# Output projection of a hybrid decoder layer: its buffers, the place of the second norm's weights, and three operands instead of four made beside it

## The chip, the cores and the metric

The kernel runs on one core of a Trainium2 chip. The metric is the device time of one execution in microseconds (us); several runs are shown by their median. One further execution was recorded by the hardware profiler, and all rows below are from that one.

## What is computed

One layer on 2048 tokens of width 1024, in float32: a norm, a projection to four mixers (a gated unit, causal pooling, sliding-window attention, stick-breaking attention), a norm of each mixer's output, the output projection with a residual, a second norm, a SwiGLU feed-forward with a residual, and a last norm.

```python
ycat = jnp.stack([y_a, y_b, y_c, y_d], axis=2)
ycat = _rmsnorm(ycat, mix_out_gain[l].reshape(N_MIXERS, GROUP_WIDTH))
x = x + ycat.reshape(B, S, D_MODEL) @ w_out[l]
h = _rmsnorm(x, norm_ffn[l])
gate, up = jnp.split(h @ w_gate_up[l], 2, axis=-1)
x = x + (jax.nn.silu(gate) * up) @ w_down[l]
return _rmsnorm(x, norm_final)
```

## The kernel before

Float32 products are made of three reduced-precision ones: each operand is split into a high part (a cast on ACT) and the rest (a subtraction on DVE), and TensorE multiplies high by high, high by rest and rest by high. The program is traced by a framework whose scheduler sets the order on each engine from its own timing model, and waits on tiles come from buffer pools: a tile of a tag that has n buffers waits until the one whose place it takes is done with.

Three parts concern us. The **output projection** (`out_proj`) goes over 16 blocks of 128 tokens. `prepare(b)` loads the mixers' rows y (L638) and the residual x (L640), squares y in four groups on ACT (L644), gets the factors from GpSimd (L145), scales y on DVE (L648), turns it by eight TensorE transposes (L630) and splits it into yT (L632 on ACT, L633 on DVE). Then 48 matmuls (L694 to L696) run in two halves, each added to the residual (L697). `finish(b)` stores the new residual, norms it (`normed`: squares L150, factor, scaling L153, written into y's buffer), turns it (L663), copies it to hs (L664) and stores that to DRAM (hTd). The program prepares block b+1 ahead of the matmuls of block b. Sliding-window attention, whose rows y the projection needs, is woven into the first half of these blocks.

The **operands of the gate product**: the feed-forward uses a Strassen-like scheme with seven operands (T2, B11, T3, T1, B21, T4, B22), sums and differences of quarters of the normed, turned rows. In `finish` of four late blocks, b1 and b2 are loaded from hTd, and `put_h` casts (L908) and splits (L909) four of the operands; B21, T4 and B22 are made by `operands` (L960 to L967) when the projection ends. All loads and stores go through one queue, that of SyncE, in order.

The **gate passes** (`gate_up`, 44 of them, 84 matmuls each, L992) and **down passes** (`down`, 88) then take their tiles from one ring, tag k4, of 18 buffers of 4 KB per partition. The projection's weights wo stand in 16 of these, and their raw rows oraw in what is left; fraw is a loaded gate weight, fsum a sum of two, fw a split one, hb and ht the rows and differences for `operands`, ar a loaded activation.

Of the kernel before, what the change touches and what calls it, by code (L numbers as in the profile page):

```python
# [68 lines left out]
def _layout(inputs):  # L69

    f = {k: np.asarray(v, dtype=np.asarray(v).dtype) for k, v in inputs.items()}
    a = {}
    x = f["x"][0]
    a["x"] = x
    a["xT"] = x.T
    w = f["w_in"][0].reshape(KT, P, 2048).transpose(1, 0, 2)

    def cols(*ranges):
        return np.concatenate([w[:, :, lo:lo + n] for lo, n in ranges], 2)

    cm = [cols((o, P)) for o in (D_K, D_Q, B_IN, B_IN + P, D_K + P, D_Q + P, C_K, C_Q, C_Q + P)]
    a["w_cm"] = np.stack(cm, 0)
    a["w_v"] = cols((D_V, 256), (C_V, P))
    a["w_a"] = cols((A_U, 512))
    a["w_out"] = f["w_out"][0]
    gu = f["w_gate_up"][0].reshape(KT, P, 2, NF, P)
    a["w_gu"] = gu.transpose(3, 1, 2, 0, 4)
    a["w_down"] = f["w_down"][0]
    for n in ("norm_mix", "mix_out_gain"):
        a[n] = f[n][0].reshape(KT, P).T  # L90
    a["norm_ffn"] = f["norm_ffn"]
    a["norm_final"] = f["norm_final"][None, :]
    a["sgu_wT"] = f["sgu_w"][0].transpose(2, 0, 1)
    a["sgu_bT"] = f["sgu_b"][0].T
    a["pool_w"] = f["pool_w"][0]
    a["pool_scale"] = f["pool_scale"]
    a["swa_sinks"] = f["swa_sinks"]
    a["rel_bias"] = f["rel_bias"]
    for n, v in _constants().items():
        a["c_" + n] = v  # L100
    return {n: np.ascontiguousarray(v) for n, v in a.items()}
# [13 lines left out]
def _build(nc, tc, A, top):  # L115
    V, S, G = nc.vector, nc.scalar, nc.gpsimd

    def load(out, in_):
        nc.sync.dma_start(out, in_)
# [26 lines left out]

    def normed(pool, x, g, out):

# [3 lines left out]
        rstd(r, ss, D, pool)  # L152
        V.scalar_tensor_tensor(out, x, r, g, op0=ALU.mult, op1=ALU.mult)  # L153

# [3 lines left out]
    with ExitStack() as ph1:  # L158
# [450 lines left out]
        def load_wo():  # L609
# [3 lines left out]
            for k in range(KT):  # L613
                raw = ring.tile([P, 2, CH], F32, name="oraw", tag="k4")
                load(raw, A["w_out"][k * P:(k + 1) * P, :].rearrange("p (n c) -> p n c", n=2))
# [19 lines left out]
        def out_proj(op, wo, put_h):  # L635
            def prepare(b):
                y = op.tile([P, D], F32, name="y", tag="y")
                load(y, yd[b // 2][(b % 2) * P:(b % 2 + 1) * P, :])  # L638
# [8 lines left out]
                for m in range(4):  # L647
                    V.tensor_scalar(y[:, m * 256:(m + 1) * 256], y[:, m * 256:(m + 1) * 256], r[:, m:m + 1], None,  # L648
                                    op0=ALU.mult)
                yT = [op.tile([P, 4, 2, P], F32R, name="yT", tag="yT", bufs=3) for _ in range(2)]  # L650
                split_T(y, yT)
                return y, xr, yT

            def finish(b, y, xr):

                load(x2d[b // 4][(b % 4) * P:(b % 4 + 1) * P, :], xr)
                normed(op, xr, gffn, y)
                hs = op.tile([P, KT, P], F32, name="hs", tag="yT", bufs=3)
                for half in range(2):
                    tr = psum.tile([P, CH], F32, name="ytr", tag="tr")  # L660
                    for k in range(4):
                        kk = half * 4 + k
                        nc.tensor.transpose(tr[:, k * P:(k + 1) * P], y[:, kk * P:(kk + 1) * P], ident)  # L663
                    S.copy(hs[:, half * 4:half * 4 + 4], tr.rearrange("p (k t) -> p k t", k=4))  # L664
                load(hTd[b // NT][:, :, b // 4 % 2, (b % 4) * P:(b % 4 + 1) * P], hs)
                k = b - NT - 1
                if 0 <= k < 4:
                    b1 = op.tile([P, 2, CH], F32, name="b1", tag="y")
                    load(b1, hTd[0][:, k])
                    b2 = op.tile([P, 2, CH], F32, name="b2", tag="xres")  # L670
                    load(b2[:, 0], hTd[0][:, 4 + k, 1])
                    put_h("B11", k, b1[:, 0])
                    V.tensor_tensor(b1[:, 0], b1[:, 1], b1[:, 0], op=ALU.subtract)
                    put_h("T1", k, b1[:, 0])
                    V.tensor_tensor(b1[:, 1], b2[:, 0], b1[:, 1], op=ALU.subtract)
# [215 lines left out]
        alone[0] = 1  # L891
        ring = top.enter_context(tc.tile_pool(name="ring", bufs=18, side="left", reuse_waits="tile"))
        wo = []
# [8 lines left out]
        with tc.tile_pool(name="ph3", bufs=2, side="right", reuse_waits="tile") as p3:  # L902
            fh = top.enter_context(tc.tile_pool(name="fh", bufs=1, side="left", reuse_waits="tile"))
            hc = {n: fh.tile([P, 4, 2, CH], F32R, name=n) for n in ("T2", "B11", "T3", "T1")}

# [4 lines left out]

            gffn = fh.tile([P, D], F32, name="gffn", tag="g")
            load(gffn, A["norm_ffn"].broadcast_to([P, D]))
            need = 0
# [13 lines left out]
    with ExitStack() as ph4:  # L927
        fp = ph4.enter_context(tc.tile_pool(name="fp", bufs=2, side="right", reuse_waits="tile"))
        for n in ("B21", "T4", "B22"):
            hc[n] = fp.tile([P, 4, 2, CH], F32R, name=n, bufs=1)  # L930
        gfin = fh.tile([P, D], F32, name="gfin", tag="g")
        load(gfin, A["norm_final"].broadcast_to([P, D]))
# [94 lines left out]
        def down(c, beside):  # L1027
            tags = (("ms", 1), ("acc", 1), ("mm", 2), ("mm", 2), ("z", 2), ("z", 2), ("tr", 2), ("tr", 2))
            pss = [psum.tile([P, CH], F32, name="dn", tag=t, bufs=n) for t, n in tags]
            for f in range(NF):  # L1030
                if f % 2 == 0:
                    ar = pair("ar")
                    for u in range(2):
                        load(ar[:, u], actd[c][f + u])
# [32 lines left out]

        for k in range(4):
            operands(0, k, ("B21", "T4", "B22"))
        for blk in range(T // TB):  # L1070
# [19 lines left out]
```

## Time and profile before

| | us |
|---|---|
| median of 3 runs | 2517.16 (2516.94 to 2519.28) |
| the profiled execution | 2518.81 |
| its span | 2517.1 |
| mean granted TensorE clock, share of full | 0.951 |
| TensorE busy | 2286.6 (91%) |
| DVE busy | 1623.0 (64%) |
| ACT busy | 1048.7 (42%) |

A busy share is a mean over stages with different limits, so the rows are by stage: where TensorE is full only fewer or faster matmuls help, and where it is not, the row to look for is the wait that ends last. [...] The turning of block 8 begins at 987.15 us, that of block 15 at 1141.06, and the first gate matmul at 1172.49.

### The profile page before, as it was taken

What the parts mean: (1) busy time and instruction counts of PE and PEld (TensorE: products, weight loads), DVE (VectorE), ACT (ScalarE), POOL (GpSimd) and SP (SyncE); (2) the same over time, 40 slices, a digit from 0 to 9 for tenths busy, and PEclk for the clock granted to TensorE, in tenths of its full rate; (3) what the DMA queues carried; (4) which work ended last, traced back from release to release, by engine and by line L of the source; (5) the groups of instructions that cost most, each with busy time, mean ns of one, the idle gap of its engine ahead of it and who ended that gap; (6) DMA issues with size and microseconds to landing.
All of it is one profiled execution on the core that took longest, in us unless ns stands there. A gap on an engine that the chain in (4) does not pass through costs nothing.

```text
span 2517.1 us, 30904 instructions
## 1 busy us (share of the span) xinstructions
PE 2286.6 (91%) x11308; PEld 1926.4 (77%) x11308; DVE 1623.0 (64%) x2634; ACT 1048.7 (42%) x2196; POOL 357.4 (14%) x372
## 2 busy tenths in 40 slices
PE   6989898897886888657999999999999999999998
PEld 6978776776875777545888888888888888888886
DVE  6688999898884543337666666655377666653443
ACT  5455566665654434234333333444233323332332
POOL 4232443454431210000000000000000000000000
PEclk9999999998996999878999999999999999999999
DMA  6232311222314333334222222556432222234553
GB/s 209 68 122 74 100 42 32 63 63 88 107 42 136 110 126 128 120 118 159 96 76 80 85 87 88 156 187 203 156 140 80 76 96 76 80 109 134 168 192 134
DMA packets 148808, 277.32 MB, mean 110 GB/s; under 512 B 12432, under 2 KB 84528, under 8 KB 148656
## 3 DMA queue, kind: packets, MB, share of 16 engines
q1 hardware_dynamic: 148656, 275.34, 32.9%
q8 instruction: 89, 1.46, 0.2%
q14 instruction: 63, 0.52, 0.1%
HBM read 211.60 MB, written 63.70 MB: 109 GB/s over the span
## 4 chain that ended last, share of the span: by engine, by line
PE 66%; DVE 15%; DMA 8%; issue 5%; ACT 3%; POOL 2%; SPq 0%; DVEq 0%; POOLq 0%; ACTq 0%
PE dn L1048 19%; PE gb L992 15%; PE gc L992 10%; PE ga L992 10%; DVE pr L315 4%; DVE s L320 3%; DMA qr<-cd 2%; DMA y<-yd 2%; DVE wt L333 1%; PE ops L694 1%; PE ops L695 1%; PE ps L242 1%; PE ps L243 1%; PE ops L696 1%; PE ps L244 1%
## 5 line engine op out<-in xcount | busy, mean ns | idle before, releaser
L1048 PE MATMUL dn<-wd,act 128*128 128x512 f32 x2112 | 479.5, 389 | 0.0
L1048 PEld LDWEIGHTS dn<-wd,act 128*128 128x128 f32 x2112 | 396.4, 188 | 82.5
L992 PE MATMUL gb<-T,fw 128*128 128x512 f32 x1584 | 387.9, 394 | 11.8 <-ACT fw L980 11.8
L992 PEld LDWEIGHTS gb<-T,fw 128*128 128x128 f32 x1584 | 298.8, 189 | 79.6 <-ACT fw L980 12.2
L992 PE MATMUL ga<-B,fw 128*128 128x512 f32 x1056 | 258.8, 393 | 0.0
L941 DVE TENSOR_TENSOR wd<-wr,wd 128x512 fp32r<-128x512 f32 x176 | 114.7, 689 | 215.4 <-ACT wd L1042 215.3
L992 PEld LDWEIGHTS ga<-B,fw 128*128 128x128 f32 x1056 | 198.6, 188 | 45.2
L145 POOL TENSOR_TENSOR fr<-rs_t,mhalf 128x1 f32<-128x1 f32 x32 | 20.3, 641 | 1449.4 <-DVE rs_t L144 1443.0
L1042 ACT CAST wd<-wr 128x512 fp32r<-128x512 f32 x176 | 101.4, 619 | 268.3 <-DMA wr<-in_w_down 242.2
L980 ACT CAST fw<-fsum 128x512 fp32r<-128x512 f32 x176 | 105.1, 620 | 200.4 <-PE gb L992 151.5
L315 DVE TENSOR_TENSOR_SCAN pr<-tfix,cr 128x513 f32<-128x513 f32 x96 | 134.3, 1406 | 11.1 <-ACT tfix L306 11.0
L213 POOL TENSOR_TENSOR h<-xr,h 128x1024 fp32r<-128x1024 f32 x47 | 122.1, 2607 | 112.1 <-ACT h L212 109.6
L992 PE MATMUL gc<-T,fw 128*128 128x512 f32 x528 | 134.1, 390 | 1.5 <-ACT fw L980 1.5
L992 PE MATMUL gc<-B,fw 128*128 128x512 f32 x528 | 130.3, 396 | 0.0
L941 DVE TENSOR_TENSOR fw<-fsum,fw 128x512 fp32r<-128x512 f32 x176 | 120.3, 687 | 11.6 <-ACT fw L980 10.0
L320 DVE TENSOR_TENSOR s<-s,pr 128x512 f32<-128x512 f32 (+3 forms) x152 | 122.8, 818 | 5.2 <-ACT s L309 1.2
L997 ACT COPY p<-gb 128x512 f32<-128x512 f32 x44 | 25.8, 585 | 227.1 <-PE gb L992 226.9
L992 PEld LDWEIGHTS gc<-B,fw 128*128 128x128 f32 x528 | 99.2, 188 | 24.0
L992 PEld LDWEIGHTS gc<-T,fw 128*128 128x128 f32 x528 | 99.2, 188 | 22.7 <-ACT fw L980 2.2
L330 PE MATMUL tr<-ident,s 128*128 128x128 f32 x544 | 97.2, 283 | 13.8 <-DVE s L320 7.7
L694 PE MATMUL ops<-wo,yT 128*128 128x512 f32 x256 | 106.8, 420 | 1.9 <-ACT yT L632 1.8
L941 DVE TENSOR_TENSOR fw<-fraw,fw 128x512 fp32r<-128x512 f32 x132 | 90.4, 687 | 26.1 <-ACT fw L980 26.1
(229 smaller groups left out, 4786.5 us busy)
## 6 DMA issues: line engine op xcount, KB each, us to landing
fraw<-in_w_gu SPq DMA_DIRECT2D x88, 512.0 KB
wr<-in_w_down SPq DMA_DIRECT2D x88, 512.0 KB
xr<-in_xT SPq DMA_DIRECT2D x48, 512.0 KB
actd<-up SPq DMA_DIRECT2D x88, 256.0 KB
ar<-actd SPq DMA_DIRECT2D x88, 256.0 KB
xt<-in_x SPq DMA_DIRECT2D x16, 512.0 KB
xres<-in_x SPq DMA_DIRECT2D x16, 512.0 KB
y<-yd SPq DMA_DIRECT2D x16, 512.0 KB
```

Source lines behind the costliest of these rows:

```text
L213: (V if q in on_v else G).tensor_tensor(h[:, :, 1], xr, h[:, :, 0].bitcast(F32), op=ALU.subtract)
L242: nc.tensor.matmul(o, w[:, 0, k], hk[:, 0], start=k == 0, stop=False)
L315: V.tensor_tensor_scan(pr[:, c0:][:, ::-1], t[:, c0:][:, ::-1], t[:, c0:][:, ::-1], carry[h][i], op0=ALU.mult, op1=ALU.bypass)
L320: (G if (4 * pair + c, i) in ON_G else V).tensor_tensor(w[:, c0:], w[:, c0:], pr[:, c0 + 1:], op=ALU.mult)
L330: nc.tensor.transpose(tr[:, i * P:(i + 1) * P], wq[i][:, col:col + P], ident)
L694: nc.tensor.matmul(ps, yk[:, 0, :], wo[k][half][:, 0], start=k == 0, stop=False)
L941: V.tensor_tensor(dst, src, hi.bitcast(F32), op=ALU.subtract)
L980: S.copy(w[:, 0], src)
L992: nc.tensor.matmul(bank, w[:, wi, sl], hc[n][:, k, hi], start=start and k + wi + hi == 0, stop=stop and k == 3 and wi == 1, skip_group_che ...
L997: S.copy(p6, bb)
L1042: S.copy(w[n][:, 0], wr[:, n])
L1048: nc.tensor.matmul(pss[2 * i + n], a[:, ai, t], w[n][:, wi], start=f + ai + wi == 0, stop=f == NF - 1 and ai == 1)
```

## The change

The rows y get three buffers (before two, shared with b1); yT gets four and hs one of its own (before three for both); b1 and b2 move to a tag `raw` with two buffers, which oraw and, later, ar use as well; the ring k4 has 16 buffers. The second norm's weights are no longer spread over all partitions and multiplied into the rows: they are one column for each group of 128 channels, and eight scaled copies of 128 columns to hs apply them (before, two plain copies of 512). T1 is no longer made beside the projection but by a loop of its own ahead of `operands`, from four more loads.

```diff
-    a["norm_ffn"] = f["norm_ffn"]
+    a["norm_ffn"] = f["norm_ffn"][0].reshape(KT, P).T
-    def normed(pool, x, g, out):
+    def normed(pool, x, out):
...
-        V.scalar_tensor_tensor(out, x, r, g, op0=ALU.mult, op1=ALU.mult)
+        V.tensor_scalar(out, x, r, None, op0=ALU.mult)
...
-                raw = ring.tile([P, 2, CH], F32, name="oraw", tag="k4")
+                raw = ring.tile([P, 2, CH], F32, name="oraw", tag="raw", bufs=2)
...
-                y = op.tile([P, D], F32, name="y", tag="y")
+                y = op.tile([P, D], F32, name="y", tag="y", bufs=3)
...
-                yT = [op.tile([P, 4, 2, P], F32R, name="yT", tag="yT", bufs=3) for _ in range(2)]
+                yT = [op.tile([P, 4, 2, P], F32R, name="yT", tag="yT", bufs=4) for _ in range(2)]
...
-                normed(op, xr, gffn, y)
-                hs = op.tile([P, KT, P], F32, name="hs", tag="yT", bufs=3)
+                normed(op, xr, y)
+                hs = op.tile([P, KT, P], F32, name="hs", bufs=1)
...
-                    S.copy(hs[:, half * 4:half * 4 + 4], tr.rearrange("p (k t) -> p k t", k=4))
+                    for k in range(half * 4, half * 4 + 4):
+                        S.activation(hs[:, k], tr[:, k % 4 * P:(k % 4 + 1) * P], AF.Copy, scale=gffn[:, k:k + 1])
...
-                    b1 = op.tile([P, 2, CH], F32, name="b1", tag="y")
+                    b1 = ring.tile([P, 2, CH], F32, name="b1", tag="raw", bufs=2)
-                    b2 = op.tile([P, 2, CH], F32, name="b2", tag="xres")
+                    b2 = ring.tile([P, 2, CH], F32, name="b2", tag="raw", bufs=2)
...
-                    put_h("T1", k, b1[:, 0])
...
-        ring = top.enter_context(tc.tile_pool(name="ring", bufs=18, side="left", reuse_waits="tile"))
+        ring = top.enter_context(tc.tile_pool(name="ring", bufs=16, side="left", reuse_waits="tile"))
...
-            hc = {n: fh.tile([P, 4, 2, CH], F32R, name=n) for n in ("T2", "B11", "T3", "T1")}
+            hc = {n: fh.tile([P, 4, 2, CH], F32R, name=n) for n in ("T2", "B11", "T3")}
...
-            gffn = fh.tile([P, D], F32, name="gffn", tag="g")
-            load(gffn, A["norm_ffn"].broadcast_to([P, D]))
+            gffn = fh.tile([P, KT], F32, name="gffn")
+            load(gffn, A["norm_ffn"])
...
-        for n in ("B21", "T4", "B22"):
+        for n in ("T1", "B21", "T4", "B22"):
-        gfin = fh.tile([P, D], F32, name="gfin", tag="g")
+        gfin = fp.tile([P, D], F32, name="gfin", bufs=1)
...
-                    ar = pair("ar")
+                    ar = ring.tile([P, 2, CH], F32, name="ar", tag="raw", bufs=2)
...
         for k in range(4):
+            b = pair("hb")
+            load(b, hTd[0][:, k])
+            V.tensor_tensor(b[:, 0], b[:, 1], b[:, 0], op=ALU.subtract)
+            put_h("T1", k, b[:, 0])
+        for k in range(4):
             operands(0, k, ("B21", "T4", "B22"))
```

The scheduler makes a new order of it. On the queue of loads and stores, around blocks 8 to 11, where yd_65 holds the rows of blocks 10 and 11, hTd_77 those from block 8 on, and the b tiles are b1 (128x1024) and b2 (128x512), the order before is:

```order
L119 DMA x2d_74<-xres 128x1024
L119 DMA xres<-in_x 128x1024
L119 DMA y<-yd_65 128x1024
L119 DMA hTd_77<-hs 1024x1x128
L119 DMA x2d_74<-xres 128x1024
L119 DMA b_10228<-hTd_76 128x512
L119 DMA b_10226<-hTd_76 128x1024
```

and of the change:

```order
L119 DMA b_10285<-hTd_76 128x1024
L119 DMA x2d_74<-xres 128x1024
L119 DMA b_10287<-hTd_76 128x512
L119 DMA xres<-in_x 128x1024
L119 DMA b_10412<-hTd_76 128x1024
L119 DMA b_10414<-hTd_76 128x512
L119 DMA y<-yd_65 128x1024
L119 DMA hTd_77<-hs 1024x1x128
```

The y ahead of the first hTd_77 was the first of the two of yd_65, block 10's; now it is the second, block 11's, and two sets of b1 and b2 stand ahead of it.

On ACT, from one finished row to the next in the blocks that make operands, the order before is:

```order
L664 COPY hs<-ytr 128x512 x2
L908 CAST B_8260<-b_10349 128x512
L908 CAST T_8262<-b_10349 128x512
L908 CAST T_8261<-b_10349 128x512
L908 CAST T_8259<-b_10351 128x512
L150 ACTIVATE y,fss<-xres 128x1024
L644 ACTIVATE junk,oss<-y 128x256 x4
L632 CAST yT<-ytr 128x4x128 x2
```

and of the change:

```order
L632 CAST yT<-ytr 128x4x128 x2
L908 CAST B_8260<-b_10285 128x512
L908 CAST T_8261<-b_10285 128x512
L908 CAST T_8259<-b_10287 128x512
L665 ACTIVATE hs<-ytr,gffn 128x128 x8
L644 ACTIVATE junk,oss<-y 128x256
L908 CAST B_8260<-b_10412 128x512
L644 ACTIVATE junk,oss<-y 128x256 x3
L908 CAST T_8261<-b_10412 128x512
L908 CAST T_8259<-b_10414 128x512
L150 ACTIVATE y,fss<-xres 128x1024
```

Two sets of casts now stand in one block, around the eight copies, and the first cast of the second set stands between the first and the second square of the next row.

On the queue in the gate passes, where actd0 and actd1 are the two stores of a pass, fraw_12650 is pass 10's before and fraw_12618 pass 10's in the change:

```order
L119 DMA actd0_8_86<-up0_12204 128x512
L119 DMA actd1_8_108<-up1_12169 128x512
L119 DMA fraw_12650<-in_w_gu 128x1024
L119 DMA fraw_12651<-in_w_gu 128x1024
L119 DMA actd0_9_87<-up0_12344 128x512
```

and of the change:

```order
L119 DMA actd0_8_86<-up0_12312 128x512
L119 DMA fraw_12618<-in_w_gu 128x1024
L119 DMA fraw_12619<-in_w_gu 128x1024
L119 DMA actd1_8_108<-up1_12277 128x512
L119 DMA actd0_9_87<-up0_12452 128x512
```

The loads for pass 10 now stand between the two stores of pass 8 instead of behind both.

## Rows read from the trace of the kernel before

**Rows 1.** Busy time by stage: stretch, its us, engines busy (x instructions), PEclk, DMA, GB/s

```profile
760.00:801.57 41.57, 24.43 (x101) 20.54 (x100) 15.59 (x26) 17.37 (x43) 7.21 (x11) 0.54 0.46 155
801.57:987.15 185.58, 158.14 (x872) 136.53 (x873) 82.67 (x166) 82.36 (x244) 31.91 (x49) 0.92 0.36 117
987.15:1141.06 153.91, 103.03 (x450) 82.96 (x450) 55.21 (x107) 47.86 (x114) 11.28 (x14) 0.82 0.39 125
1141.06:1172.49 31.43, 15.26 (x73) 12.12 (x73) 21.29 (x36) 12.60 (x24) 1.54 (x2) 0.75 0.72 248
1172.49:2517.10 1344.61, 1332.89 (x5808) 1092.20 (x5808) 798.43 (x1269) 456.81 (x840) 10.67 (x16) 1.00 0.35 118
```

**Rows 2.** The same view of one late block

```profile
1023.11:1049.61 26.50, 14.66 (x64) 11.74 (x65) 10.79 (x21) 7.80 (x20) 2.42 (x3) 0.76 0.40 136
```

**Rows 3.** Waits (us in total, times, longest): late stage twice, then attention stage

```profile
PE ytr L630 <- DVE y L648: 42.0, 4, 11.8
...
SPq L119 <- PE ytr L663: 61.1, 7, 13.6
...
PE ytr L630 <- DVE y L648: 11.0, 3, 7.8
```

**Rows 4.** Chain of waits, 1064 to 1078: start us, us, what

```profile
1065.23 1.21 DVE T L909 x2
1066.47 4.21 DMA y<-yd
1070.76 0.52 ACT junk L644 x2
```

**Rows 5.** Timeline at block 15's turning: start us, us, engine, line, operation

```profile
1139.03 0.19 ACT L644 ACTIVATION_READ_ACCUMULATOR junk<-y 128x1 f32 x1
1139.61 0.39 PE L695 MATMUL ops<-wo,yT 128*128 128x512 f32 x1
1139.84 0.39 PE L696 MATMUL ops<-wo,yT 128*128 128x512 f32 x1
1141.06 1.20 PE L630 MATMUL ytr<-ident,y 128*128 128x128 f32 x8 [0.83 <-issue]
1142.39 0.50 PE L694 MATMUL ops<-wo,yT 128*128 128x512 f32 x1
```

**Rows 6.** The same view, block 9's finished row being turned

```profile
1013.99 1.03 PE L663 MATMUL ytr<-ident,y 128*128 128x128 f32 x8
1014.62 1.08 ACT L664 COPY hs<-ytr 128x512 f32<-128x512 f32 x2 [6.49 <-PE ytr L663]
1014.78 0.48 PE L696 MATMUL ops<-wo,yT 128*128 128x512 f32 x1
```

**Rows 7.** The same view, ACT early in the program: a scaled copy, and what follows

```profile
33.35 0.37 ACT L285 ACTIVATE vstack<-ps,rx 128x128 fp32r<-128x128 f32 x1
33.62 0.39 ACT L271 CAST dq<-sc 64x256 fp32r<-64x256 f32 x1
```

**Rows 8.** Instructions of L153: xcount, duration ns min/median/max

```profile
L153 DVE SCALAR_TENSOR_TENSOR y<-xres,fr,gffn x16: 1276/1284/1747, 836.7 to 1157.4; 128x1024 f32<-128x1024 f32 x16
```

**Rows 9.** Timeline of the changeover to the gate products

```profile
1160.43 0.69 DVE L960 TENSOR_TENSOR ht<-hb 128x512 f32<-128x512 f32 x1 [1.80 <-DMA hb<-hTd]
1161.37 0.53 SPq L119 DMA_DIRECT2D hTd<-hs  x1
1165.62 0.62 ACT L908 CAST T<-ht 128x512 fp32r<-128x512 f32 x1 [3.76 <-DMA hTd<-hs]
1172.49 1.22 PE L992 MATMUL gb<-T,fw 128*128 128x512 f32 x2 [11.76 <-ACT fw L980]
```

**Rows 10.** Timeline of one gate pass: load, first cast, its first product

```profile
1405.79 0.98 SPq L119 DMA_DIRECT2D fraw<-in_w_gu  x2
1413.07 0.62 ACT L980 CAST fw<-fsum 128x512 fp32r<-128x512 f32 x1 [0.28 <-DVE fsum L976]
1417.00 2.88 PE L992 MATMUL gb<-T,fw 128*128 128x512 f32 x12
```

## Prediction, made before the changed kernel was run

> **What bounds the kernel now.** I read the busy shares by stage first, then the waits inside the stage that stands out, then the chain of waits there. By stage [rows 1] TensorE is busy for 1332.89 of 1344.61 us from 1172.49 us on (the feed-forward part, granted clock 1.00), so nothing outside TensorE can be saved there. In the output projection it is not: 103.03 of 153.91 us between the turning of block 8 (987.15) and of block 15 (1141.06), at a mean granted clock of 0.82, and 15.26 of the 31.43 us of the changeover. Between 801.57 and 987.15, where attention runs beside it, it is busy for 158.14 of 185.58 us. One late block, 1023.11 to 1049.61, holds 14.66 us of TensorE in 26.50, with DVE at 10.79 and ACT at 7.80 [rows 2]: no engine is full, so a chain of waits sets the time.
>
> Which chain, the waits say [rows 3]: in 987.15 to 1141.06 TensorE stood 42.0 us in 4 waits for the scaled row y (L648) before it could turn it, and the DMA queue stood 61.1 us for the turning of an older row (L663). The chain of waits shows one link in a row [rows 4]: the last work on the difference operands (L909 to 1066.44), then at once the load of the next y (1066.47, 4.21 us), then its squares. That is a buffer: y has two, b1 takes one of them, and the load waits until it is given back.
>
> **The change part by part.** I go by the profiled execution, 2518.81 us (span 2517.1), which is 1.65 above the median of 2517.16.
>
> *Three y buffers, b1 and b2 elsewhere.* In the queue, the load of block b+3's row now stands ahead of block b's store of hs, where before it was block b+2's: one block earlier, with nothing of the operands in its buffer. The 4.21 us of loading and the wait before it leave the path. What comes next has to be worked out, since the period does not fall to TensorE's own work.
> TensorE alone, a block at full clock: turning y to the first projection matmul 1.33 us (1141.06 to 1142.39, [rows 5]); 48 matmuls at 0.23 (1139.61 to 1139.84) is 11.0; the eight transposes of the finished row 0.79 (1013.99 to 1014.78, [rows 6]): 13.2 in all, 92 for seven blocks.
> The next bound: on ACT, block b+1's four squares stand behind the eight scaled copies of block b-1 (the fence on ACT), and those wait for L663, which the new order puts n matmuls into block b. From L663: 0.63 to the first copy [rows 6]; eight copies; four squares at 0.52, 2.1 [rows 4]; 1.84 from the end of the last square (1139.22) to the next turning (1141.06, [rows 5]). A copy of this form (128x128 from PSUM, scaled by a column) took 0.37 and the next instruction began after 0.27 [rows 7], so eight take 2.3 where the two copies now take 1.08 [rows 6]. Sum 6.9, and a block is 1.33 + 0.23n + 6.9. By the order n is 41 in block 8 (while attention ends) and 25, 28, 24, 32, 25, 32 in 9 to 14: 17.7 us for block 8, 13.8, 15.6, 14.0 and 15.6 for 11 to 14.
> Blocks 9 and 10 make the operands, two sets in each, and the second set's first cast stands between the first and the second square. Its b1 can be loaded only when the first set has left the raw buffer. With the first b1 landing about 4.5 us into the block, a cast and subtractions of 0.6 each [rows 4], it is free at 8; 4.2 for the load, 0.6 for the cast, 1.6 for three squares, 1.84, and some 0.6 behind DVE's own subtractions: 17 us each. If the loads were hidden it would be 15, if they miss once more 21.
> Sum 17.7 + 17 + 17 + 13.8 + 15.6 + 14.0 + 15.6 = 111 us. TensorE's busy 103.03 against its 92 at full clock says that the lower clock, which here follows the long idle times, costs 10.6 us now; waits of 1 to 4 us remain, so I leave 3 of it: 114. **-39 us**, from -61 (TensorE's 92) to -24 (17.3 for a plain block, with the two of the operands at 21).
>
> [...]
>
> *Own buffers for turned rows and hs.* Before, the next block's two turned tiles and hs rotate through three buffers. TensorE hardly waits for that now (its waits are for y), so I give it nothing of its own; it is what lets y be turned a block ahead.
>
> *The norm without its weights on DVE.* L153 took 1.284 us with two tensor operands [rows 8]; one operand fewer cannot make it longer, and L663 follows it by several matmuls in the order. Nothing, save at the changeover, where it shortens the tail by 0 to 0.7 and the eight copies lengthen it by 1.2.
>
> *Attention beside it, 801.57 to 987.15.* 11.0 us of waits for y go [rows 3]. DMA and softmax waits of attention stand in the same TensorE queue and can take their place, and each block gets 1.2 us more ACT. I take **-7**, from -14 (with the clock that returns) to +4.
>
> *Start.* The weights of the projection are now staged through two buffers and the first y loads queue behind them: **+1**, from 0 to 4.2, one load of 512 KB [rows 4].
>
> *T1 made at the changeover.* Twelve loads of hb instead of eight, 16 casts instead of 12. The last two hb follow hs of block 15 in the queue. Before, the last hb is not what the store of hs (1161.37) waits for, and ACT waits 3.76 for that store, to 1165.62 [rows 9]. After: issue 0.6 after the store, landing 4.2 to 5 later, say 1166.4; then DVE has 17 operations in a row at 0.605 [rows 4] before the first fsum is whole (the new first subtraction of that last hb stands ahead of 14 splits): 1177.4, one cast, and the first gate matmul at 1178 where it was 1172.49. **+6**, from -2 (all of T1 in the 3.76 us of ACT's wait, DVE ahead) to +10. The work that T1 cost in blocks 9 to 12 is part of the block sums above.
>
> *A ring of 16, not 18; ar in the raw buffers.* Rows of the gate weights are loaded just in time: issued at 1405.79, their sum cast by 1413.69, and used by TensorE at 1417.00, a margin of 3.3 us [rows 10]. In the new order the load for pass 10 stands between the two stores of pass 8, not behind both and just ahead of pass 9's: earlier, not later. What hides it is that margin and TensorE's full 19 us a pass. **0**; a lost margin is the slower rival.
>
> Sum: -39 - 7 + 1 + 6 = -39, or 2479.8 for the profiled execution and **2478** for the median.
>
> **The rivals.**
> 1. *TensorE becomes the bound in the late blocks*: the copies and squares run ahead and a block is 13.2. For it: ACT has room (7.80 of 26.50 [rows 2]). Against: the squares stand behind the copies in ACT's order. -61 - 11 + 1 + 4 = -67: 2450.
> 2. *The new wait is longer*: blocks of 17.3 and a clock that still falls, attention taking up what y gives, a changeover of +8 to +10. -24 - 3 + 2 + 9 = -16, up to 2501; I put it at 2497.
> 3. *Slower: the smaller ring starves the gate passes.* If a load comes as late as two tiles fewer make it (11 tiles in 19.3 us, so 1.76 each, 3.5) and another 0.9 for a store ahead of it in the queue, 4.4 against the margin of 3.3 leaves 1.1 in each of 44 passes, 48 us: 2526. It decides from 39/44 = 0.9 us a pass. Against: the new order has the load earlier.
> 4. *The change does not bring the row earlier*: y stands behind b1 and b2 in the one queue, so the waits on y in operand blocks move to those loads, and blocks 11 to 14 save little more than the changeover takes. 2517 within 5.
>
> **How the numbers follow.** Forecast (2465 to 2490) 0.53; rival 1 0.15; rival 2 0.22; rival 3 0.05; rival 4 0.05. The range 2455 to 2498 leaves out part of rivals 1 and 2 and all of 3 and 4, 2 in 10. Of this kernel a measurement can tell about 0.2% (5 us) from no change. Faster by more: the forecast, rivals 1 and 2 and a little of rival 4, 0.91; within it 0.03; slower 0.06.
>
> **What would show it.** Right: waits of TensorE on L648 in the late blocks fall from 42.0 to under 15; loads of y landing well ahead of their squares; blocks of 14 to 16 us with granted clock near 0.95; the wait for the first gate cast at 16 to 19 where it is 11.76; TensorE still full after it. Wrong: a late block under 13.5 (rival 1) or over 17 with ACT waiting for b (rival 2); idle TensorE with the load of fraw as releaser (rival 3).

## The result, and the profile after

The changed kernel takes 2477.99 us, the median of 4 runs (2475.26 to 2478.93), against 2517.94 (2516.94 to 2519.28, 4 runs) for the kernel before: a ratio of 0.9839, 95% interval 0.9822 to 0.9856. It is faster by 40 us, where 2478 had been forecast. The profiled execution has a span of 2475.9 us against 2517.1, so 41.2 us have to be found in the stages.

The same cuts as in [rows 1] are, after the change, the turning of block 0 (802.16), of block 8 (976.48), of block 15 (1088.62) and the first gate matmul (1129.30). The view is that of the engines' busy time by stage, of the changed kernel:

```profile
760.00:802.16 42.16, 23.99 (x105) 21.24 (x105) 18.27 (x31) 18.77 (x46) 6.14 (x10) 0.54 0.48 153
802.16:976.48 174.32, 151.38 (x846) 129.45 (x847) 78.01 (x163) 86.91 (x280) 31.70 (x50) 0.91 0.39 125
976.48:1088.62 112.14, 99.47 (x469) 80.39 (x467) 48.60 (x101) 53.06 (x155) 11.63 (x14) 0.95 0.49 158
1088.62:1129.30 40.68, 16.58 (x72) 13.30 (x72) 27.10 (x47) 15.95 (x40) 1.10 (x2) 0.68 0.78 269
1129.30:2475.90 1346.60, 1336.22 (x5808) 1092.36 (x5808) 804.26 (x1265) 465.56 (x840) 11.94 (x16) 1.00 0.35 118
```

Row by row against [rows 1]: start +0.6, attention stage -11.3, late blocks -41.8, changeover +9.3, the rest +2.0; together -41.2. In the late stage TensorE is now busy for 99.47 of 112.14 us at a granted clock of 0.95, where it was 103.03 of 153.91 at 0.82.

The waits of that stage (who waited for whom, us in total, times, longest; 976.48 to 1088.62) answer to [rows 3]:

```profile
ACT hs L665 <- PE ytr L663: 26.3, 5, 6.7
...
PE ytr L630 <- issue: 6.2, 4, 2.0
...
PE ytr L630 <- ACT T L908: 5.9, 2, 3.4
```

TensorE's 42.0 us of waiting for the scaled row (L648) are gone. What is left are 5.9 us in the two blocks that make operands, and 6.2 of waits for which the view names nothing. The timeline of the changed kernel at the end of block 13 says what stands behind these (start us, us, engine, line, operation):

```profile
1066.53 1.03 PE L663 MATMUL ytr<-ident,y 128*128 128x128 f32 x8
...
1067.17 2.17 ACT L665 ACTIVATE hs<-ytr,gffn 128x128 f32<-128x128 f32 x8 [6.71 <-PE ytr L663]
...
1069.18 0.44 ACT L644 ACTIVATE junk<-y 128x256 f32<-128x256 f32 x1
...
1071.17 0.19 ACT L644 ACTIVATION_READ_ACCUMULATOR junk<-y 128x1 f32 x1
...
1071.39 0.17 DVE L144 TENSOR_SCALAR rs_t<-oss 128x4 f32<-128x4 f32 x1 [0.77 <-ACT junk L644]
...
1071.71 1.02 POOL L145 TENSOR_TENSOR orr<-rs_t,mhalf 128x4 f32<-128x4 f32 x1 [12.11 <-DVE rs_t L144]
...
1072.76 1.14 DVE L648 TENSOR_SCALAR y<-y,orr 128x256 f32<-128x256 f32 x4 [1.20 <-POOL orr L145]
...
1073.22 0.98 PE L630 MATMUL ytr<-ident,y 128*128 128x128 f32 x6 [0.37 <-issue]
```

This is the chain that the prediction gave for the new period: the turned row of the block before (L663), 0.64 later eight copies, then the four squares of the next row at once, and 1.86 us from their end to the next turning. No square waits for a load here: the row being squared was loaded from 1052.54 on, 16 us earlier.

The changeover, same view, in place of [rows 9]:

```profile
1104.27 0.69 DVE L961 TENSOR_TENSOR ht<-hb,ht 128x512 f32<-128x512 f32 x1 [0.54 <-DMA hb<-hTd]
1104.88 0.68 DVE L697 TENSOR_TENSOR xres<-ops,xres 128x512 f32<-128x512 f32 x1
...
1111.92 0.52 SPq L119 DMA_DIRECT2D hTd<-hs  x1
...
1117.49 0.69 DVE L960 TENSOR_TENSOR ht<-hb 128x512 f32<-128x512 f32 x1 [2.04 <-DMA hb<-hTd]
...
1127.85 0.69 DVE L976 TENSOR_TENSOR fsum<-fsum,fraw 128x512 f32<-128x512 f32 x1
...
1129.30 1.22 PE L992 MATMUL gb<-T,fw 128*128 128x512 f32 x2 [18.81 <-ACT fw L980]
```

From the store of block 15's hs 5.57 us pass to the last hb, then DVE has a row of subtractions until the first fsum is whole at 1128.54, and TensorE has waited 18.81 us where it waited 11.76.

### The profile page after: what moved, and what is told of

Same layout as the page of the kernel before. It is cut to its first block, busy times and chain, and to the rows that moved or that the text cites. A ratio compares the mean times of both kernels' runs of the same rounds, so it can differ in the third digit from the quotient of the medians.

```text
span 2475.9 us, 31097 instructions
## 1 busy us (share of the span) xinstructions
PE 2276.8 (92%) x11308; PEld 1912.9 (77%) x11308; DVE 1622.2 (66%) x2638; ACT 1072.1 (43%) x2292; POOL 356.1 (14%) x372
## 4 chain that ended last, share of the span: by engine, by line
PE 54%; DVE 1%; issue 0%; DMA 0%; ACT 0%; DVEq 0%; POOL 0%; ACTq 0%; SPq 0%; POOLq 0%
PE dn L1048 19%; PE gb L992 15%; PE gc L992 10%; PE ga L992 10%; DMA hb<-hTd 0%; DVE B L909 0%; DVE xa L1058 0%; DVE T L909 0%; DVE xa L1056 0%; ACT hs L665 0%; DVEq L1091 0%; POOL fr L145 0%; DVE fsum L976 0%; DVE ht L961 0%; ACT fw L980 0%
## 5 line engine op out<-in xcount | busy, mean ns | idle before, releaser
L145 POOL TENSOR_TENSOR fr<-rs_t,mhalf 128x1 f32<-128x1 f32 x32 | 20.8, 654 | 1414.0 <-DVE rs_t L144 1408.5
L315 DVE TENSOR_TENSOR_SCAN pr<-tfix,cr 128x513 f32<-128x513 f32 x96 | 134.3, 1406 | 10.5 <-ACT tfix L306 10.3
L980 ACT CAST fw<-fraw 128x512 fp32r<-128x512 f32 x132 | 81.3, 620 | 63.3 <-DVE fw L941 31.8
L306 ACT ACTIVATE tfix<-z 128x512 f32<-128x512 f32 (+3 forms) x160 | 86.1, 538 | 47.1 <-PE z L303 34.2
```

Of the source, the lines that this page charges most:

```text
L145: G.tensor_tensor(out, t, mhalf[:, :k], op=ALU.pow)
L306: S.activation(t[:, c0:CH], z[:, :n], AF.Sigmoid, scale=-0.125)
L315: V.tensor_tensor_scan(pr[:, c0:][:, ::-1], t[:, c0:][:, ::-1], t[:, c0:][:, ::-1], carry[h][i], op0=ALU.mult, op1=ALU.bypass)
L980: S.copy(w[:, 0], src)
```

## The experiments

Times of one profiled execution by stage, in us, cut as above; the ratio is that of the timed runs to those of the kernel before on the same chip (whose median lay between 2514.6 and 2520.6), with its 95% interval.

| kernel | attention | late | changeover | rest | median | ratio |
|---|---|---|---|---|---|---|
| before | 185.58 | 153.91 | 31.43 | 1344.61 | | 1 |
| after | 174.32 | 112.14 | 40.68 | 1346.60 | 2477.99 | 0.9839 (0.9822 to 0.9856) |
| y2 | 177.42 | 121.53 | 44.77 | 1346.67 | 2494.33 | 0.9915 (0.9900 to 0.9930) |
| yt3 | 175.28 | 112.41 | 40.98 | 1346.51 | 2477.65 | 0.9848 (0.9833 to 0.9863) |
| t1_yt3 | 175.25 | 113.96 | 34.65 | 1344.55 | 2468.02 | 0.9810 (0.9796 to 0.9825) |
| rows | 173.29 | 111.19 | 42.70 | 1347.26 | 2478.99 | 0.9851 (0.9834 to 0.9867) |
| b_raw | 191.85 | 130.98 | 39.10 | 1344.10 | 2510.33 | 0.9959 (0.9947 to 0.9972) |
| b_in_y | 173.83 | 116.00 | 40.27 | 1346.49 | 2481.46 | 0.9868 (0.9854 to 0.9883) |
| rows_y2 | 190.41 | 126.80 | 44.37 | 1347.16 | 2514.87 | 0.9996 (0.9987 to 1.0006) |
| dve4 | 168.55 | 110.02 | 38.75 | 1346.60 | 2467.62 | 0.9796 (0.9774 to 0.9818) |
| early | 173.22 | 114.04 | 14.89 | 1365.89 | 2474.28 | 0.9821 (0.9802 to 0.9840) |
| t1_early | 174.88 | 114.13 | 13.27 | 1354.53 | 2463.79 | 0.9779 (0.9756 to 0.9802) |
| t1_early_dve4 | 165.78 | 110.59 | 13.22 | 1357.14 | 2452.03 | 0.9748 (0.9734 to 0.9763) |
| best_dvex | 168.35 | 110.20 | 13.36 | 1358.54 | 2453.49 | 0.9754 (0.9738 to 0.9770) |

The part ahead of 800 us, which no edit but the staging of the projection's weights touches, ends between 797.4 and 805.3 in these executions; two kernels with the same edits there (t1_yt3 and t1_early) differ by 7.6. So a few us of a single total say nothing, and the stages are compared instead.

**Which of the buffers: y2, b_in_y, b_raw, rows_y2.** y2 takes the third buffer of y away:

```diff
-                y = op.tile([P, D], F32, name="y", tag="y", bufs=3)
+                y = op.tile([P, D], F32, name="y", tag="y", bufs=2)
```

> The changed kernel with two buffers for the rows y instead of three; b1 and b2 stay where the change put them. Theory A (what mattered is that b1 no longer takes a buffer of y): blocks of before that made no operands already took 15.6 to 18.7 us with two buffers, so the late stage (turning of block 8 to that of block 15) stays within 112 to 122 us against the 112.14 of the changed kernel, 2478 to 2488 in all. Theory B (the third buffer is what brings the row in time): blocks go back towards 25 us, the late stage to 140 or more, 2505 or more, with TensorE's waits for y (L648) back at 30 us or more.

2494.33 us: neither theory. The late stage, 121.5, is at theory A's upper end, and the whole is above it. In the blocks without operands the load of y is back on the chain, in parallel with the copies and longer than they are. The queue's row and ACT's, of y2 in block 12 (timeline):

```profile
1060.29 0.32 SPq L119 DMA_DIRECT2D y<-yd  x1
```

```profile
1059.86 2.17 ACT L665 ACTIVATE hs<-ytr,gffn 128x128 f32<-128x128 f32 x8 [8.09 <-PE ytr L663]
1063.87 0.39 ACT L644 ACTIVATE junk<-y 128x256 f32<-128x256 f32 x1 [1.83 <-DMA y<-yd]
```

The load can only be issued when L663 has read the old row out of the buffer, and the first square waits 1.83 us longer than the copies took. The order of y2 differs in part from that of the changed kernel, but in blocks 12 and 14 L663 stands 32 matmuls into the block in both: these blocks take 18.95 and 17.47 us where the changed kernel takes 15.40 and 15.40. b_in_y keeps the three buffers and gives b1 and b2 their old places:

```diff
-                    b1 = ring.tile([P, 2, CH], F32, name="b1", tag="raw", bufs=2)
+                    b1 = op.tile([P, 2, CH], F32, name="b1", tag="y", bufs=3)
...
-                    b2 = ring.tile([P, 2, CH], F32, name="b2", tag="raw", bufs=2)
+                    b2 = op.tile([P, 2, CH], F32, name="b2", tag="xres")
```

> The changed kernel with b1 back in a buffer of y (which keeps three) and b2 back in one of xres, as before the change. Theory A (b1's place in y's buffers is the larger part): with one of three taken the operand blocks grow from 17 to 18 to 21 us, the plain ones stay at 15, the late stage is 118 to 128 us, and the whole 2484 to 2494. Theory I (the number of buffers left for y is all that counts, and two are enough in operand blocks): late stage within 4 us of 112, the whole within 4 of the changed kernel's 2478.

A late stage of 116.0, 3.9 above the changed kernel, and a ratio 0.003 higher: the edge of theory I, and less than theory A wanted. b1's place is the smaller part, once y has three buffers. (The order spreads the operands' casts over blocks 9 to 13 here, so the place is not all that changed.) b_raw is the reverse, the kernel before with the raw buffers alone (oraw and ar, whose lines are left out here, use them too):

```diff
-                    b1 = op.tile([P, 2, CH], F32, name="b1", tag="y")
+                    b1 = ring.tile([P, 2, CH], F32, name="b1", tag="raw", bufs=2)
...
-                    b2 = op.tile([P, 2, CH], F32, name="b2", tag="xres")
+                    b2 = ring.tile([P, 2, CH], F32, name="b2", tag="raw", bufs=2)
...
-        ring = top.enter_context(tc.tile_pool(name="ring", bufs=18, side="left", reuse_waits="tile"))
+        ring = top.enter_context(tc.tile_pool(name="ring", bufs=16, side="left", reuse_waits="tile"))
```

> The kernel before with one part of the change alone: b1 and b2 (and oraw, ar) in two raw buffers, the ring at 16. y keeps two buffers, now its own; T1 is made beside the projection, the weights are on the rows, hs and yT share three buffers. Theory A (b1's place in y's buffers is the cause): operand blocks fall from 25 us to 16 to 20, the late stage from 153.9 to 118 to 130, and the whole to 2482 to 2495, close to y2 (2494). Theory F (it takes the third buffer or the norm's change as well): operand blocks stay above 22 us and the whole above 2503.

Where the kernel before made the operands in four blocks of 24.8 to 26.5 us (10 to 13, one set each), b_raw makes them in two (9 and 10, two sets each) of 20.0 and 20.8. The late stage falls by 23 us, close to theory A's bound, but attention (+6.3), the changeover (+7.7) and the start (+3.7, within its scatter) give most of it back: ratio 0.9959. Neither theory foresaw both, and no run here shows why attention and changeover grew. rows_y2 has two y buffers and the weights on the rows:

```diff
-                y = op.tile([P, D], F32, name="y", tag="y", bufs=3)
+                y = op.tile([P, D], F32, name="y", tag="y", bufs=2)
...
-        V.tensor_scalar(out, x, r, None, op0=ALU.mult)
+        V.scalar_tensor_tensor(out, x, r, g, op0=ALU.mult, op1=ALU.mult)
...
-                    for k in range(half * 4, half * 4 + 4):
-                        S.activation(hs[:, k], tr[:, k % 4 * P:(k % 4 + 1) * P], AF.Copy, scale=gffn[:, k:k + 1])
+                    S.copy(hs[:, half * 4:half * 4 + 4], tr.rearrange("p (k t) -> p k t", k=4))
```

> The changed kernel with two buffers for y and with the weights on the rows and two plain copies. It lies between y2 (2494, weights as scaled copies) and b_raw (2510, which also makes T1 beside and shares hs with yT). Theory J (with two buffers for y, the scaling of the finished row on DVE, 1.28 instead of 0.74 us, is on the chain that frees y's buffer, and with it the order changes): 2503 to 2510. Theory K (T1 beside the projection makes the difference): 2491 to 2497.

Its ratio, 0.9996, is that of no change at all. With the weights on the rows the third buffer is therefore worth 36 us (2514.87 against 2478.99), with the weights on the turned rows 16 (2494.33 against 2477.99; 19 by the ratios), and with two buffers the place of the weights is worth 20. In the profiled executions, whose spans differ by 18 us, 13 are in the attention stage and 5 in the late one (table). Waits of TensorE in the attention stage, first of rows_y2, then of y2:

```profile
PE ytr L663 <- DVE yT L633: 7.2, 3, 2.9
...
PE o L487 <- DMA block<-vd: 5.8, 2, 3.3
```

```profile
PE o L487 <- DMA block<-vd: 1.9, 2, 1.6
PE ytr L663 <- DVE yT L633: 1.6, 1, 1.6
```

The first fits a longer L153: the turning of the finished row waits for DVE, where L153 stands ahead of the L633 named, and with two buffers the next load of y waits for that turning. It gives 5.6 of the 13; the second gives 3.9. The scheduler's order differs too (the second half of L663 stands 20 matmuls into most blocks of that stage, not 18), and no run here holds it still, so how the 20 us divide between the longer L153 and the order is open.

**Own buffers for yT and hs: yt3.**

```diff
-                yT = [op.tile([P, 4, 2, P], F32R, name="yT", tag="yT", bufs=4) for _ in range(2)]
+                yT = [op.tile([P, 4, 2, P], F32R, name="yT", tag="yT", bufs=3) for _ in range(2)]
...
-                hs = op.tile([P, KT, P], F32, name="hs", bufs=1)
+                hs = op.tile([P, KT, P], F32, name="hs", tag="yT", bufs=3)
```

> The changed kernel with hs and the turned rows yT sharing three buffers again, as before the change. Theory A (their own buffers are worth nothing, as the prediction had it): late stage 112 within 4 us, 2478 within 4. Theory C (they are what lets y be turned a block ahead): the cast of yT waits for a store of hs, 2 to 3 us a block, the late stage 126 to 135 us, 2490 to 2500.

Every stage is within 1 us of the changed kernel but the start. Theory A holds: these 8 KB per partition buy nothing.

**T1 back beside the projection: t1_yt3.** The room that yt3 frees is enough for T1's tile:

```diff
-            hc = {n: fh.tile([P, 4, 2, CH], F32R, name=n) for n in ("T2", "B11", "T3")}
+            hc = {n: fh.tile([P, 4, 2, CH], F32R, name=n) for n in ("T2", "B11", "T3", "T1")}
...
+                    put_h("T1", k, b1[:, 0])
...
-        for k in range(4):
-            b = pair("hb")
-            load(b, hTd[0][:, k])
-            V.tensor_tensor(b[:, 0], b[:, 1], b[:, 0], op=ALU.subtract)
-            put_h("T1", k, b[:, 0])
```

> As yt3 (hs and yT share three buffers), and T1 made beside the projection again, from b1, as before the change; the loop for T1 at the changeover is gone. Theory A (b1's place is what mattered; T1's work beside is cheap): the wait for the first gate cast falls from 18.8 to 12 or 13 us, the late stage grows by 1 to 5 us over that of yt3, the whole is 3 to 6 us below yt3. Theory D (the late blocks became short because T1's casts and subtractions left them): late stage 125 us or more, and the whole 5 us or more above yt3.

The wait for the first gate cast is 13.1 us; against yt3 the late stage grows by 1.6, the changeover falls by 6.3 and the rest by 2.0. Theory D falls: T1's work had hardly cost anything in the late blocks, and moving it out cost 8 us behind them. (The median is 9.6 lower; 2.3 of the profiled difference lie in the start.)

**The copies on the chain: rows and dve4.** rows takes the eight copies back to two, with three y buffers; its diff is the second and third part of that of rows_y2.

> The changed kernel with the second norm's weights multiplied into the rows on DVE again and two plain copies of 512 columns to hs, as before the change, in place of the eight scaled copies. Theory A (the copies stand on the chain of the late blocks, block = 1.33 + 0.23 n + 6.9 with 2.3 for the copies): 1.1 us less in each of seven late blocks and some 0.3 less at the changeover, 2468 to 2472 if the order stays. Theory E (the copies lie beside other work, the period has another cause): 2478 within 3.

2478.99, as theory E said. But the scheduler had moved L663: it now stands, in turn, 45 and 18 matmuls into a block, where it was 32 and 25. With copies of 1.08 the prediction's block is 1.33 + 0.23n + 5.7, 17.4 us for n = 45, and the two such blocks took 17.16 and 16.96; the others, with 41 and 40 matmuls of the projection in them, took 13.32 and 11.73, of which TensorE was busy for 13.18 and 11.59. So the chain was shorter and the order spent the gain, which leaves theory E unsupported as well. dve4 shortens the copies in another way, and here L663 keeps its place in blocks 12 to 14:

```diff
                     for k in range(half * 4, half * 4 + 4):
-                        S.activation(hs[:, k], tr[:, k % 4 * P:(k % 4 + 1) * P], AF.Copy, scale=gffn[:, k:k + 1])
+                        if half:
+                            V.tensor_scalar(hs[:, k], tr[:, k % 4 * P:(k % 4 + 1) * P], gffn[:, k:k + 1], None, op0=ALU.mult)
+                        else:
+                            S.activation(hs[:, k], tr[:, k % 4 * P:(k % 4 + 1) * P], AF.Copy, scale=gffn[:, k:k + 1])
```

> The changed kernel with the second four of the eight scaled copies to hs made by DVE instead of ACT. Theory A (the copies stand on ACT ahead of the next squares: block = 1.33 + 0.23 n + 6.9): blocks with n = 32 fall from 15.4 to 14.3, those with n of 22 to 25 stop at TensorE's 13.2 to 13.8 (now 14.6 and 15.06), block 8, with n at 24 instead of 41, from 17.9 to 14; the late stage falls from 112.1 to 104 to 108 us, the whole to 2470 to 2475. Theory E (copies are hidden): blocks with n = 32 stay at 15.4, 2477 to 2480 but for block 8.

Blocks 14 and 12, with n = 32 as in the changed kernel, took 14.42 and 14.43 us instead of 15.40, and block 13, with n = 25, 13.34: theory A, to a tenth or two. (Block 8 took 14.85 for an expected 14, and block 11, behind the operands, stayed at 14.73.) That the late stage is 110.0 and not 104 to 108 comes from the two operand blocks, 19.34 and 18.91, 2 us longer each. In block 9 the order has L663 at 32 matmuls instead of 25, in block 10 at 28 in both. TensorE's wait there (dve4, waits in 985 to 1024 us) is for DVE again, on which the copies now stand beside the operands' subtractions; whether the copies or the order make the 2 us is not shown:

```profile
PE ytr L630 <- DVE y L648: 8.9, 2, 6.0
```

The whole is below theory A's range for another reason. Of the 10 us that the profiled spans of dve4 and the changed kernel differ by, the late stage gives 2.1, the changeover 1.9 and the attention stage 5.8. The order in the attention stage is another one too, and no run here parts it from the shorter copies, so dve4 shows the copies' price in blocks 12 to 14 and not in the 10 us.

**The changeover: early and t1_early.** In early the products with T2, B11 and T3 of the first gate pass come ahead of the loops that make the other four operands:

```diff
             product(bb, s3, "T3", False, True)
+            if rest:
+                rest()
...
-                gate_up(blk, f)
+                gate_up(blk, f, rest if blk + f == 0 else None)
```

(rest holds the two loops, which are gone from their old place.)

> The changed kernel with the first gate pass begun before T1, B21, T4 and B22 are made: its products with T2, B11 and T3, which exist by then, come ahead of the two loops in the program. Theory G (the changeover is 40.7 us because the first sum of gate weights stands behind 16 splits on DVE): the first gate matmul comes 9 to 13 us earlier, 36 matmuls (8.3 us) run beside the splits, 2464 to 2471. Theory H (the operands' own work, loads of hb until 1117 and splits until 1127, sets the end whatever comes first): TensorE stops again ahead of the T1 product and 2474 to 2478 remains.

The first gate matmul comes at 1104.81, 24 us earlier, and theory H is right all the same: changeover and rest are 1380.78 together against 1387.28, a gain of 6.5 (the ratios, 0.9821 and 0.9839, have intervals that overlap). Timeline of TensorE in early:

```profile
1110.25 1.03 PE L663 MATMUL ytr<-ident,y 128*128 128x128 f32 x8
1113.64 3.02 PE L992 MATMUL gb<-T,fw 128*128 128x512 f32 x12 [2.35 <-ACT p L997]
1132.69 1.22 PE L992 MATMUL gc<-T,fw 128*128 128x512 f32 x2 [16.04 <-ACT fw L980]
```

The 36 matmuls are done by 1117, and the product with T1 waits 16.04 us, by this view not for T1 but for the cast of its gate weights. ACT's timeline in early has that cast behind those of the operands, which wait for DVE's differences:

```profile
1130.46 0.62 ACT L908 CAST T<-ht 128x512 fp32r<-128x512 f32 x1 [3.88 <-DVE ht L962]
1130.98 1.13 ACT L908 CAST B<-hb 128x512 fp32r<-128x512 f32 x2
1132.02 0.61 ACT L980 CAST fw<-fsum 128x512 fp32r<-128x512 f32 x1
```

A version with that cast ahead of the operands was not run.

t1_early is the same edit on t1_yt3, where rest holds only the loop for B21, T4 and B22.

> As t1_yt3 (T1 beside the projection, hs and yT share three buffers, the rest as changed), with the first gate pass begun before B21, T4 and B22 are made. Theory G: the first gate matmul comes 7 to 11 us earlier than in t1_yt3, with 48 matmuls (11 us) beside the splits; 2457 to 2462. Theory H: TensorE stops again ahead of the B21 product; 2465 to 2469.

Changeover and rest are 1367.80 against 1379.20 in t1_yt3: 11.4 less, theory G by the stages; the whole, 0.0031 or 8 us lower by the ratios, lies between the two theories. TensorE still waits 6.05 and 1.76 us ahead of the T1 product.

**Together: t1_early_dve4 and best_dvex.**

> As t1_early, with the second four of the eight scaled copies to hs on DVE. Theory A (the copies' chain sets the plain blocks, here too): plain late blocks of 13.3 to 14.4 us, block 8 at 15; with the gain of dve4 (10 us below the changed kernel) on that of t1_early (14 below), 2452 to 2458. Theory L (DVE's subtractions for the operands, of which there are more with T1 beside, give the gain back in blocks 9 and 10): 2459 to 2464.

> As t1_early_dve4, but in finishing blocks 9 and 10 all eight copies stay on ACT, since dve4's operand blocks had grown by 2 us each. If DVE's four copies are what made them grow: 2 to 5 us below t1_early_dve4. If not: within 2 us of it.

t1_early_dve4 is the best kernel here: 2452.03 us, ratio 0.9748, 63 us below the kernel before and 23 below the changed one by the ratios. Its blocks 12 to 14 took 13.36, 14.42 and 13.36 us, as theory A said. The total of theory L is not met, but in part it is right: blocks 9 to 11 take 54.6 us where t1_early takes 52.1. Again the larger part of the gain over t1_early, 9.1 of the 12.3 us between the profiled spans, is in the attention stage. best_dvex leaves all copies on ACT in finishing blocks 9 and 10,

```diff
-                        if half:
+                        if half and not 9 <= b < 11:
```

and is the same within its interval. The copies of a finished row run one block later, so by its trace it is blocks 10 and 11 that have all eight on ACT; block 9 still has four on DVE. Block 10, which makes operands, took 18.48 us against 19.03, so DVE's copies cost it some 0.6 us at most. Block 9 took 18.63 against 17.73, and block 11 15.98 against 17.83, with L663 at 25 matmuls instead of 31. What lengthens block 9 was not tested.

## Why the prediction was right, step by step

**Late blocks**, forecast 114, measured 112.14. Block 8 was to take 17.7 and took 17.87, the operand blocks 17 each and took 16.84 and 16.97, blocks 11 to 14 were to take 13.8, 15.6, 14.0 and 15.6 and took 14.60, 15.40, 15.06 and 15.40. The chain is the one that was named, and dve4, at the same n, shortened the period by 0.98 us, half of the 2.01 that the eight copies take. Rival 1 falls, for TensorE's 13.2 was not reached until the copies were split; but it was near, since in blocks 11 and 13 TensorE was busy for 14.45 of 14.60 and 14.69 of 15.06 us, at a mean granted clock of 0.90 and 0.89 (in blocks 12 and 14 it was busy for 13.29 and 13.26 at 1.00). Rivals 2 and 4 fall too: no late block but block 8 took over 17 us, and no square of the late blocks waits for a load of y. Block 13 shows why the short blocks miss the formula. Busy time and granted clock (PEclk, third from the end) of the changed kernel, at the start of block 13, then at that of block 12:

```profile
1058.16:1061.50 3.34, 3.34 (x12) 2.61 (x13) 2.61 (x7) 1.29 (x4) 0.55 (x1) 0.55 0.32 129
...
1042.76:1046.00 3.24, 3.11 (x16) 2.40 (x17) 2.72 (x7) 2.18 (x4) 0.05 (x1) 1.00 0.35 143
```

Ahead of block 13 TensorE stood idle for 1.98 us, and its first 12 instructions (eight transposes and four matmuls) ran at a granted clock of 0.55; ahead of block 12 nothing shows as idle, and the clock stayed at 1.00. (In stretches of 1 us from 750 to 1150 us of this trace the clock is 1.00 in 274, 0.50 in 108 and between the two in 18.) The fifth matmul starts 3.37 us into block 13 and 2.36 into block 12, and the chain then waits for L663, later by this 1.0 us. The 3 us left for this were about right: with the measured 2.01 for the copies in place of 2.3 the formula gives 109, and 112.14 was measured.

**What carried it** was named only in part. The prediction put the gain on one edit, three buffers and b1's new place, with b1 in y's buffer as the cause seen in [rows 4]. That cause is there (b_raw: 41 us in two operand blocks instead of 102 in four), but b_raw alone brings a ratio of 0.9959; with three buffers b1 may stay where it was for 0.003 more. The third buffer is what counts, worth 36 or 16 us, each time with the order that the scheduler then made.

**The weights off DVE**, put at nothing, are worth nothing with three buffers (rows, with another order) and 20 us with two (y2 against rows_y2), the copies that go with them included. The step was right for this change and would have been wrong for a smaller one. That the third buffer is what hides L153 is not shown, since how much of the 20 us is L153 and how much the order is open.

**Attention stage**, -7 forecast, -11.3 measured, inside its bounds. Waits of TensorE in that stage, after the change:

```profile
PE o L487 <- DMA block<-vd: 9.6, 4, 5.7
PE ops L694 <- ACT yT L632: 7.6, 2, 7.4
...
PE ytr L630 <- DVE y L648: 0.9, 3, 0.4
```

The 11.0 us of waits for y fell to 0.9, as forecast, and other waits did take their place in part: that for attention's rows vd was 5.2 before, and that for the turned row yT was none. TensorE's idle time fell by 4.5 us only (185.58 - 158.14 before, 174.32 - 151.38 after). The other 6.8 us are less busy time: 26 instructions fewer stand in this stage (872 and 846), while the late blocks have 19 more (450 and 469). So some of the 11.3 is work that now lies on the other side of the cut. **Start**, +1 forecast, +0.6 measured, which is less than the scatter of that part and confirms nothing.

**Changeover**, +6 forecast, +9.3 measured. The part behind the store was right: 5.57 to the last hb (forecast 5.0), then 11.05 us of DVE until the first sum (forecast 11). The 11 is a slip, though: 17 operations at 0.605 are 10.3, and the trace has 18. Mis-sized was the tail of block 15, from its turning to the store of hs: 23.30 us instead of 20.31. The prediction's text gave it 0.5 to 1.2 more, by the longer copies and the shorter L153, and its sum nothing. A granted clock of 0.58 in its first 4.05 us (1.00 in the first 4.04 before) makes 1.2 of the 3.0 (14.64 instead of 13.45 to the last matmul's end). Another 1.6 is the second half's addition (L697), whose sums were whole at 1103.26 and which started at 1104.88, behind L961 waiting for hb on DVE. The copies add 0.8, and the shorter L153 takes 0.5 off.

**Ring of 16**, 0: t1_yt3 has the ring of 16 and ar in the raw buffers and needs 1344.55 us from the first gate matmul on, where the kernel before needs 1344.61. Rival 3 falls. The +2.0 has another source (below). **Own buffers for yT and hs**, 0: yt3 shows the same. The prediction's remark that they let y be turned a block ahead is wrong: yt3 lacks them and takes the same time.

**The total** is closer than its parts, and that is luck. The late blocks (-41.8 for -39) and attention gave 3 and 4 us more than forecast, the changeover and the feed-forward part took 3 and 2 back. The -39 itself is 114 less 153.91, which is -39.9.

On the eight copies, [rows 7] gave 2.3 us by the spacing. The trace now has 2.01 from the start of the first copy to that of the first square (1067.17 to 1069.18), 0.3 less.

## What to carry to other kernels

Where an engine waits for a row in a ring of buffers, write down the whole loop that gives a buffer back, every engine and queue in it, and compute the period that the next loop would have; here that gave each block to about a microsecond, given the order that the scheduler had made. Edits on such a loop are not additive: what one is worth depends on whether another has already taken the loop off the path, so undo them one at a time and in pairs. Price work that is moved out of a busy stage to a changeover where TensorE stands still: here T1 was nearly free beside the projection (the late stage grew by 1.6 us) and cost 8 us behind it (6.3 in the changeover, 2.0 after it).

## What the runs showed of the hardware

The +2.0 us in the feed-forward part is in the matmuls: TensorE is busy for 3.3 us more (1332.89 and 1336.22) with the same 5808 instructions. Groups of instructions from 1150 us on (count, busy us, mean ns of one), of b_raw, the changed kernel and t1_yt3:

```profile
L992 PE MATMUL gc<-T,fw 128*128 128x512 f32 x528 | 128.4, 390 | 0.9 <-ACT fw L980 0.9
```

```profile
L992 PE MATMUL gc<-T,fw 128*128 128x512 f32 x516 | 128.3, 396 | 0.0
```

```profile
L993 PE MATMUL gc<-T,fw 128*128 128x512 f32 x516 | 124.8, 389 | 0.0
```

These are the products with T1; busy time over count is 243, 249 and 242 ns. (The kernel before has 390 ns too, but a busy time of 134.1 us, since its products come in another order.) One takes 389 or 390 ns where T1's tile is in the pool of T2, B11 and T3 (before, b_raw, t1_yt3) and 396 where it is in that of B21, T4 and B22 (after, y2, yt3, rows, b_in_y); the stage is 1344.1 to 1344.6 us in the first and 1346.5 to 1347.3 in the second. Same instruction, same shapes, other place in memory: some 0.1% of the kernel. That the place is the cause is argued from these kernels, none of which changes the place alone. What it is about the place is open.

Scaling a row of 128x1024 on DVE took 1.284 us with two tensor operands [rows 8] and 0.753 with one (L153 after the change, median of 16).
